# The adaLN gates of a two-layer decoder: broadcast by unit-column matmuls, or written to memory and read back into every partition

## The chip, the cores and the metric

One core of one Trainium2 chip runs the whole program; the other cores idle. The metric is the device time of one execution in microseconds. TensorE (PE in the profile, PEld for its weight loads) multiplies; VectorE (DVE) and ScalarE (ACT) copy, add, scale and split operands; GpSimd (POOL) does gathers and small work; SyncE (SP) issues nearly all loads of weights. A DMA that SP issues stands in one queue of instructions with its waits: while SP waits for one, what stands behind it isn't issued.

## The reference, cut to what matters

There are two layers. In each, a token mixer (layer 0: sparse attention, layer 1: a gated linear recurrence) and then a mixture of 16 experts are added to the residual stream `x` of 512 tokens by 1024 channels. Each of the four sub-layers has its own shift, scale and gate from the conditioning vector `c`:

```
mod = silu(c) @ ada_w[l, s] + ada_b[l, s]      # 3 x 1024 numbers: shift, scale, gate
h   = rms_norm(x, gain) * (1 + scale) + shift
x   = x + gate * mixer(h)                      # gate: one number for each of the 1024 channels
```

The gate has 1024 numbers for the whole sequence, the same for every token. Here a token is a partition, so the gate has to stand in every partition.

## The kernel before

All products are float32 and are made as three products of split operands (`hi`, `lo`): ACT copies the high part (`whi`, `ohi`), DVE subtracts it (`wlo`, `olo`), and PE adds hi·hi, hi·lo and lo·hi.

**Where the gates come from.** `ada_parts(l, s)` (L161) is the matrix product of `c` with `ada_w[l, s]` in six parts of 512 columns, each with a 2 MB load on SP (L88) and 32 matmuls (L181). Parts 4 and 5 are the gate. Their result lies in four partitions (0, 32, 64, 96) of 128 channels each, and DVE adds it to the bias in `gg` (L187). The parts are spread over the mixers as filling work; the next part's weights are loaded when a buffer is free, which a later part's matmuls or a later split decides.

**Where the gates are used.** `mix_out` (L1698) is the output stage of a mixer: `out_proj` (L357) multiplies the mixer's output `ot` by `w_out` (L373 to L375: hi·hi, hi·lo and lo·hi of the splits, for K tiles 0 to 7), four token tiles by two column halves. It begins with K tiles 0 to 6 of token tiles 0 and 1, stops at a `yield`, and gets the gate by `rest.send(...)`. Then comes K tile 7 of tiles 0 and 1, and for each tile of tokens the residual: DVE multiplies the PSUM bank by the gate (`yres`, L406) and adds it to `x` (L407). The splits of token tile 2 (`ohi` on ACT, L367, and `olo` on DVE, L368) reuse the buffers of tile 0, so ACT waits for tile 0's last hi·lo product. Behind the output stage come the norm, the router and the expert lists of the mixture (`route`), and then the experts.

**What makes the broadcast.** `gate_row` (L213) takes one half of a gate: four matmuls, of a unit column of `ident` repeated 128 times by `gg`, put 512 gate values into all 128 partitions of a PSUM tile `gate_ps` (L217; each float32 matmul runs as two, so the trace has 8 for a half). `gate_tokens` (L221) copies the mixer's gate to `gateb`, 128x1024, by two DVE copies (L224). `Moe.gate` (L1425) does it for the gate of the experts and keeps two layouts: `gate64` (DVE, L1435) and `gate32` (ACT, L1437), which the experts' outputs are multiplied by (L1534).

**The order.** `mix_out` first queues the loads of the first expert weights, `m.load(EARLY, m.early)` (L1226 and L1230 on SP), then the first part of `out_proj`, `m.prepare()` (the small matmuls L1194 and L1201), `m.gate()` and `gate_tokens`. A scheduler then orders the instructions of each engine.

Of the kernel before, what the change touches and what calls it, by code (L numbers as in the profile page):

```python
# [9 lines left out]
F32 = mybir.dt.float32  # L10
# [3 lines left out]
AF = mybir.ActivationFunctionType  # L14
# [4 lines left out]
D = 1024  # L19
# [12 lines left out]
EARLY = 3  # L32
# [27 lines left out]
def kernel(ctx: ExitStack, tc: tile.TileContext, I, out, dbg=None, upto="all"):  # L60
    nc = tc.nc
# [5 lines left out]
    dram = ctx.enter_context(tc.tile_pool(name="dram", bufs=1, space=bass.MemoryType.DRAM))  # L67
    psum = ctx.enter_context(tc.tile_pool(name="psum", bufs=1, space=bass.MemoryType.PSUM))

    def sb(name, side="left", bufs=1):  # L70
        return tc.tile_pool(name=name, bufs=bufs, side=side, reuse_waits="tile")

    def mm_ps(name):
        return psum.tile([128, 512], F32, tag="mm", bufs=3, name=name)

    def tp_ps(name):
        return psum.tile([128, 512], F32, tag="tp", bufs=3, name=name)
# [8 lines left out]
    def load_w(src, pool=ring, eng=nc.sync):  # L86
        w = pool.tile([128, 8, 512], F32, tag="w", name="w")
        loads.append(eng.dma_start(out=w, in_=src))  # L88
        return w
# [8 lines left out]
    ident = const.tile([128, 128], F32, name="ident")  # L98
# [45 lines left out]
    def side_by_side(makes):  # L144

        first = last = makes[0]()
        for make in makes[1:]:
            with tc.high_priority(offset=TOGETHER):
                ins = make()
            edge(ins, last)  # L150
            last = ins
        return first
# [3 lines left out]
    gates = {}  # L156
# [4 lines left out]
    def ada_parts(l, s):  # L161

        aw = I["ada_w"][l, s]
        mod = const.tile([128, 16], F32, name=f"mod{l}{s}")
        gg = const.tile([128, 2, 128], F32, name=f"gg{l}{s}")
        mods[l, s] = mod
        gates[l, s] = gg

        def load(t, wpool, eng):
            if t == 4:  # L170
                nc.gpsimd.memset(gg, 0.0)
                nc.scalar.dma_start(out=gg[0:128:32],
                                    in_=bass.AP(tensor=I["ada_b"].tensor,
                                                offset=I["ada_b"].offset + 3 * D * (2 * l + s) + 2 * D,
                                                ap=[[128, 4], [512, 2], [1, 128]]))
            return load_w(aw[:, 512 * t:512 * t + 512].rearrange("(k p) n -> p k n", p=128), wpool, eng)

        def part(t, w):
            ps = mm_ps("ada_ps")
            for q in range(0, NK, 2):  # L180
                side_by_side([lambda k=k, g=g: nc.tensor.matmul(  # L181
                    ps[32 * g:32 * g + 32, 0:128], cond[:, k:k + 1].to_broadcast([128, 32]),
                    w[:, k, 128 * g:128 * g + 128], start=(k == 0), stop=(k == NK - 1))
                    for k in (q, q + 1) for g in range(4)])
                yield
            if t >= 4:
                nc.vector.tensor_add(gg[:, t - 4], gg[:, t - 4], ps[:, 0:128])  # L187
                return
            row = small.tile([128, 128], F32, tag="adarow", bufs=2, name="adarow")
            nc.vector.tensor_copy(row, ps[:, 0:128])  # L190
            tp = tp_ps("ada_tp")
            nc.tensor.transpose(tp[:, 0:128], row, ident)
            b0 = (2 * l + s) * 24 + 4 * t
            m4 = mod[:, 4 * t:4 * t + 4]
            nc.vector.tensor_add(m4, tp[:, 0:128:32], cols[:, b0:b0 + 4])
            if t >= 2:
                g0 = 96 + (2 * l + s) * 8 + 4 * (t - 2)
                nc.vector.scalar_tensor_tensor(m4, m4, 1.0, cols[:, g0:g0 + 4], op0=ALU.add, op1=ALU.mult)

        return [(lambda wpool=ring, eng=nc.sync, t=t: load(t, wpool, eng), lambda w, t=t: part(t, w)) for t in range(6)]  # L200

    def in_turn(parts, ahead, wpool=ring):
# [7 lines left out]
        for part, w in q:  # L210
            yield from part(w)

    def gate_row(gg, t):  # L213

        ps = tp_ps("gate_ps")
        for g in range(4):
            nc.tensor.matmul(ps[:, 128 * g:128 * g + 128], ident[:, 32 * g:32 * g + 1].to_broadcast([128, 128]),  # L217
                             gg[:, t, :], start=True, stop=True)
        return ps

    def gate_tokens(pool, gg):  # L221
        gb = pool.tile([128, D], F32, tag="gateb", bufs=1, name="gateb")
        for t in range(2):
            nc.vector.tensor_copy(gb[:, 512 * t:512 * t + 512], gate_row(gg, t))  # L224
        return gb


# [187 lines left out]
    def nsa(l, load, src, m, ada0, fill):  # L415
        win = I["nsa_w_in"][0]
        with ExitStack() as st:
            with ExitStack() as s2:
                ot, wts = nsa_heads(l, load, win, m, s2, ada0, fill)
            dump("ot", ot)  # L420
            mix_out(l, m, ot, wts, src)
# [472 lines left out]
    def hgrn(l, m0, st0, fill):  # L894
        win = I["hgrn_w_in"][0]
        with ExitStack() as st:
# [31 lines left out]
            def begun(st):  # L928
                st.push(wst)
                return got[0]  # L930

            mix_out(l, m, ot, None, None, begun)
        return m

# [232 lines left out]
    class Moe:  # L1167
# [257 lines left out]
        def gate(self):  # L1425

            self.gate_of = {m: self.pool.tile([128, 8 * m], F32, name=f"gate{m}") for m in (64, 32)}
            for t in range(2):
                ps = gate_row(gates[self.l, 1], t)
                for m, g in self.gate_of.items():  # L1430
                    for j in range(128 // m):
                        if 8 * m * j // 512 == t:
                            r, c = slice(m * j, m * j + m), 8 * m * j % 512
                            if m == 64:
                                nc.vector.tensor_copy(g[r], ps[r, c:c + 8 * m])  # L1435
                            else:
                                nc.scalar.activation(g[r], ps[r, c:c + 8 * m], AF.Copy)  # L1437

        def slot_tokens(self, p):
            if p < PINS:  # L1440
# [260 lines left out]
    def mix_out(l, m, ot, wts, src, front=None):  # L1701

        if src is not None:
            xp = m.under.enter_context(sb("mx"))
            m.x = [xp.tile([128, D], F32, name=f"x{t}") for t in range(NT)]
        m.early = m.left.enter_context(sb("moew0", side="right", bufs=EARLY))
        m.load(EARLY, m.early)
        with ExitStack() as st:
            rest = front(st) if front else out_begin(st, ot, wts)
            wk = st.enter_context(sb("mixo"))  # L1710
            m.work = wk
            m.prepare()
            m.gate()
            rest.send((wk, gate_tokens(wk, gates[l, 0]), src, m.x, m.tokens))
            m.load(2, ring)

    def out_begin(st, ot, wts, scale=None):
        g = out_proj(st.enter_context(sb("mixw")), ot, wts, scale)
        next(g)
        return g  # L1720
# [8 lines left out]
    def moe_out(pool, m, t):  # L1729
# [4 lines left out]
        return m.x[t]  # L1734

    ada = {(l, s): ada_parts(l, s) for l in range(2) for s in range(2)}
    first = ada[0, 0][0:4]
    fill = ada[0, 0][4:6] + ada[0, 1] + ada[1, 0][0:4]
# [90 lines left out]
```

## Time and profile before

| | |
|---|---|
| three runs | 1449.33, 1451.39 and 1454.22 us, median 1451.39 us |
| the profiled execution | 1452.37 us, span 1450.4 us |
| mean granted clock of TensorE | 0.947 of full speed |
| PE busy | 1280.3 us, 88% of the span |
| DVE busy | 714.7 us, 49% |
| ACT busy | 428.9 us, 30% |
| DMA | 346.47 MB, mean 239 GB/s |

Start times are microseconds from the start of the profiled span; the span is 1.97 us shorter than that execution's time. Layer 0's output stage lies at about 419 to 485 us and layer 1's at about 1080 to 1145; the experts of layer 0 run from about 500 us, those of layer 1 from about 1165.

### The profile page before, as it was taken

Reading aid. Unit: us, or ns where it says so; the run is one execution under the profiler, and the core shown is the slowest. Engines: PE = TensorE matmul, PEld = TensorE weight load, DVE = VectorE, ACT = ScalarE, POOL = GpSimd, SP = SyncE. Lnnn points to the kernel's source line nnn. Section 1 sums busy time; section 2 is a strip of 40 time slices with the busy share of each in tenths; the row PEclk is TensorE's granted clock in tenths of the full one; section 3 lists DMA queues with packets and bytes.
Section 4 is the critical chain, followed back from the end, with each engine's and each line's share of the span. In section 5 each row is a group of like instructions: output and inputs, shape, how many; then the busy total and the mean of one; then the engine's idle time right before and its main releaser. Section 6 shows DMA issues by size and latency. Waiting matters only on the chain. (4 is left out here: it accounts for less than half of the span.)

```text
span 1450.4 us, 26217 instructions
## 1 busy us (share of the span) xinstructions
PE 1280.3 (88%) x10634; PEld 773.9 (53%) x10635; DVE 714.7 (49%) x1801; ACT 428.9 (30%) x1007; POOL 154.2 (11%) x174
## 2 busy tenths in 40 slices
PE   5998898988989699999983999999889699999991
PEld 3666655765557443443322867777667533444320
DVE  4435886458846732222217465666555652222213
ACT  3323565336643121111114422233233221111110
POOL 2102212221100100000004100000000110000002
PEclk9999999999999799999995999999889899999996
DMA  9802551734373799999996333353335689999995
GB/s 358 221 1 85 181 187 62 289 123 155 118 315 135 264 339 394 370 374 371 402 364 195 101 105 130 118 175 117 118 117 232 236 312 389 376 378 385 387 387 190
DMA packets 108335, 346.47 MB, mean 239 GB/s; under 512 B 17251, under 2 KB 40635, under 8 KB 87724
## 3 DMA queue, kind: packets, MB, share of 16 engines
q1 hardware_dynamic: 77632, 276.80, 50.9%
q0 software_dynamic: 10048, 38.54, 8.0%
q10 hardware_dynamic: 20524, 29.34, 5.9%
q8 instruction: 87, 1.43, 0.4%
q14 instruction: 44, 0.36, 0.1%
HBM read 320.73 MB, written 23.93 MB: 238 GB/s over the span
## 5 line engine op out<-in xcount | busy, mean ns | idle before, releaser
L1491 PE MATMUL h_ps<-w,hgt 128*32 128x256 f32 (+1 forms) x2240 | 325.5, 492 | 6.5 <-DMA w<-in_moe_w_dram 6.5
L1491 PEld LDWEIGHTS h_ps<-w,hgt 128*32 128x32 f32 (+1 forms) x2240 | 110.8, 124 | 196.8 <-issue 160.5
L1531 PE MATMUL y_ps<-w,gT 128*64 128x512 f32 (+1 forms) x1120 | 158.2, 485 | 1.1 <-ACT gT L1520 1.1
L1509 DVE TENSOR_TENSOR go<-h_ps,g 32x256 f32<-32x256 f32 (+1 forms) x70 | 58.9, 841 | 134.5 <-ACT g L1507 134.2
L313 PE MATMUL pr_ps<-whi,hThi 128*128 128x512 f32 x256 | 107.5, 421 | 2.9 <-DVE qn L518 1.8
L1531 PEld LDWEIGHTS y_ps<-w,gT 128*64 128x64 f32 (+1 forms) x1120 | 55.9, 123 | 89.6 <-issue 75.8
L314 PE MATMUL pr_ps<-wlo,hThi 128*128 128x512 f32 x256 | 102.7, 401 | 0.0
L315 PE MATMUL pr_ps<-whi,hTlo 128*128 128x512 f32 x256 | 102.3, 400 | 0.1
L1534 DVE TENSOR_TENSOR y<-y_ps,gate 128x512 f32<-128x512 f32 (+1 forms) x52 | 31.2, 599 | 136.7 <-PE y_ps L1531 134.1
L1507 ACT ACTIVATE g<-h_ps 64x512 f32<-64x512 f32 (+1 forms) x52 | 26.8, 516 | 229.1 <-PE h_ps L1491 166.6
L303 DVE TENSOR_TENSOR wlo<-w,whi 128x512 fp32r<-128x512 f32 x120 | 80.2, 703 | 23.9 <-ACT whi L302 20.5
L1473 DVE TENSOR_SCALAR hgt<-hg_tp,modp 128x96 f32<-128x96 f32 (+2 forms) x128 | 43.5, 366 | 97.1 <-PE hg_tp L1465 91.6
L302 ACT ACTIVATE whi<-w 128x512 fp32r<-128x512 f32 x120 | 71.9, 631 | 64.6 <-DMA w<-in_nsa_w_in_dram 16.5
L802 ACT ACTIVATE P<-P,nm 128x128 f32<-128x128 f32 (+3 forms) x128 | 71.0, 556 | 38.9 <-DVE nm L800 37.7
L181 PE MATMUL ada_ps<-w,cond 128*32 128x128 f32 x1536 | 64.9, 297 | 15.4 <-DMA w<-in_ada_w_dram 9.6
L796 PE MATMUL s_ps<-kT,qT 128*128 128x256 f32 (+3 forms) x256 | 66.0, 364 | 11.4 <-DVE qn L518 6.9
L800 DVE CUSTOM_DVE_ANT_0 P<-s_ps,tb 128x128 f32<-128x128 f32 (+3 forms) x128 | 59.6, 486 | 22.0 <-PE s_ps L796 18.3
L1520 ACT ACTIVATE gT<-g_tp 128x384 f32<-128x384 f32 (+2 forms) x32 | 14.6, 457 | 165.5 <-PE g_tp L1517 156.8
L1453 POOL DMA_INDIRECT hg<-xnd,gidxp x26 | 23.6, 906 | 363.2 <-PE hg_tp L1465 360.6
L841 PE MATMUL p_tp<-ident,P 128*128 128x128 f32 x320 | 52.7, 282 | 8.1 <-DVE P L816 8.0
L1471 ACT ACTIVATE hgt<-hg_tp,modp 128x96 f32<-128x96 f32 (+2 forms) x128 | 47.9, 420 | 40.6 <-DVE hgt L1473 36.7
L181 PEld LDWEIGHTS ada_ps<-w,cond 128*32 128x32 f32 x1536 | 42.2, 117 | 31.5 <-issue 23.8
(367 smaller groups left out, 2102.9 us busy)
## 6 DMA issues: line engine op xcount, KB each, us to landing
w<-in_moe_w_dram SPq DMA_DIRECT2D x120, 1024.0 KB
w<-in_moe_w_dram SPq DMA_DIRECT2D x32, 2048.0 KB
w<-in_ada_w_dram SPq DMA_DIRECT2D x22, 2048.0 KB
w<-in_hgrn_w_in_dram SPq DMA_DIRECT2D x12, 1024.0 KB
tb<-tabd ACTq DMA_DIRECT2D x16, 456.0 KB
yd<-y ACTq DMA_DIRECT2D x56, 128.0 KB
yd<-zero POOLq DMA_DIRECT2D x12, 512.0 KB, 8.7
w<-in_nsa_w_in_dram SPq DMA_DIRECT2D x8, 512.0 KB
```

The source lines that it names most:

```text
L181: side_by_side([lambda k=k, g=g: nc.tensor.matmul(ps[32 * g:32 * g + 32, 0:128], cond[:, k:k + 1].to_broadcast([128, 32]), w[:, k, 128 * g ...
L302: nc.scalar.activation(a, w[:, k], AF.Copy)
L303: nc.vector.tensor_sub(b, w[:, k], a.bitcast(F32))
L313: nc.tensor.matmul(ps, hi[:, k, c], a, start=(k == 0), stop=False)
L314: nc.tensor.matmul(ps, hi[:, k, c], b, start=False, stop=False)
L315: nc.tensor.matmul(ps, lo[:, k, c], a, start=False, stop=(k == NK - 1))
L796: nc.tensor.matmul(sp[:, :n], qT[:, (hd + j) % 8, 128 * t:128 * t + 128], kT[:, v, br, gl, :n], start=(v == 0), stop=(v == 1))
L800: nc.vector.tensor_tensor_reduce(ps, sp[:, :n], tbs[hd + j][:, 384 - 128 * t:512], scale=-1.0, scalar=3.0e38, op0=ALU.add, op1=ALU.min, ac ...
L802: nc.scalar.activation(ps, ps, AF.Exp, bias=nm[:, i:i + 1], scale=-1.0, accum_out=z[:, i:i + 1])
L1491: self.pe(nc.tensor.matmul(ps[m * j:m * j + m, :w], hgt[:, k, r:r + m], ws[half][:, x + i, c:c + w], start=(k == 0), stop=(k == NK - 1)))
L1509: nc.vector.tensor_mul(go[r:r + m].rearrange("q (f p) -> q p f", f=4)[:, 2 * m * j:2 * m * j + 2 * m], ps[64 + m * j:64 + m * j + m, :w].r ...
L1531: self.pe(nc.tensor.matmul(ps[m * j:m * j + m, :w], gT[:, f, r:r + m], w2v[:, f, w * j:w * j + w], start=(f == 0), stop=(f == 3)))
```

## The change

The result of each gate part is written to a small DRAM tile `gd` by SP right after DVE's add, 4 partitions of 128 values (2 KB). Where a gate is needed in every partition, SP reads it back with a partition step of 0: once for `gateb` (512 KB), six times for the two layouts of the experts' gate (two of 64 partitions by 512 values, four of 32 by 256). `gate_row`, its matmuls and the copies out of PSUM are gone. In `mix_out` both gates now come before the first loads of expert weights in the code.

```diff
@@ ada_parts
         gg = const.tile([128, 2, 128], F32, name=f"gg{l}{s}")
+        gd = dram.tile([2, 4, 128], F32, name=f"gd{l}{s}")
         mods[l, s] = mod
-        gates[l, s] = gg
+        gates[l, s] = gd
...
             if t >= 4:
                 nc.vector.tensor_add(gg[:, t - 4], gg[:, t - 4], ps[:, 0:128])
+                nc.sync.dma_start(out=gd[t - 4], in_=gg[0:128:32, t - 4])
                 return
...
-    def gate_row(gg, t):
-
-        ps = tp_ps("gate_ps")
-        for g in range(4):
-            nc.tensor.matmul(ps[:, 128 * g:128 * g + 128], ident[:, 32 * g:32 * g + 1].to_broadcast([128, 128]),
-                             gg[:, t, :], start=True, stop=True)
-        return ps
-
-    def gate_tokens(pool, gg):
+    def gate_load(dst, gd, c, n):
+
+        nc.sync.dma_start(out=dst, in_=bass.AP(tensor=gd.tensor, offset=gd.offset + c, ap=[[0, dst.shape[0]], [1, n]]))
+
+    def gate_tokens(pool, gd):
         gb = pool.tile([128, D], F32, tag="gateb", bufs=1, name="gateb")
-        for t in range(2):
-            nc.vector.tensor_copy(gb[:, 512 * t:512 * t + 512], gate_row(gg, t))
+        gate_load(gb, gd, 0, D)
         return gb
@@ Moe.gate
             self.gate_of = {m: self.pool.tile([128, 8 * m], F32, name=f"gate{m}") for m in (64, 32)}
-            for t in range(2):
-                ps = gate_row(gates[self.l, 1], t)
-                for m, g in self.gate_of.items():
-                    for j in range(128 // m):
-                        if 8 * m * j // 512 == t:
-                            r, c = slice(m * j, m * j + m), 8 * m * j % 512
-                            if m == 64:
-                                nc.vector.tensor_copy(g[r], ps[r, c:c + 8 * m])
-                            else:
-                                nc.scalar.activation(g[r], ps[r, c:c + 8 * m], AF.Copy)
+            for m, g in self.gate_of.items():
+                for j in range(128 // m):
+                    gate_load(g[m * j:m * j + m], gates[self.l, 1], 8 * m * j, 8 * m)
@@ mix_out
-        m.load(EARLY, m.early)
         with ExitStack() as st:
             rest = front(st) if front else out_begin(st, ot, wts)
             wk = st.enter_context(sb("mixo"))
             m.work = wk
+            gateb = gate_tokens(wk, gates[l, 0])
+            m.gate()
+            m.load(EARLY, m.early)
             m.prepare()
-            m.gate()
-            rest.send((wk, gate_tokens(wk, gates[l, 0]), src, m.x, m.tokens))
+            rest.send((wk, gateb, src, m.x, m.tokens))
             m.load(2, ring)
```

Line numbers of the changed kernel are 3 to 10 lower than those of the kernel before in what follows (L365 is the old L368, L403 the old L406, L1223 the old L1226). Two places show how the engines' order moves. The first is SP late in layer 1's mixer, from the last load of `ada_w` to the loads of expert weights (`moe_w`). Before:

```order
L88 DMA w<-in_ada_w_dram 128x8x512
L88 DMA w<-in_hgrn_w_out_dram 128x8x512 x2
L1226 DMA w<-in_moe_w_dram 128x2048 x6
L1230 DMA w<-in_moe_w_dram 128x4096
L1226 DMA w<-in_moe_w_dram 128x2048 x2
```

After (`gd_117` and `gate_...` belong to the experts' gate of layer 1, `gd_114` and `gateb` to its mixer's gate):

```order
L88 DMA w<-in_ada_w_dram 128x8x512
L189 DMA gd_117<-gg_116 4x128
L88 DMA w<-in_hgrn_w_out_dram 128x8x512
L217 DMA gate_10654<-gd_117 64x512
L217 DMA gate_10655<-gd_117 32x256 x2
L88 DMA w<-in_hgrn_w_out_dram 128x8x512
L189 DMA gd_117<-gg_116 4x128
L217 DMA gate_10654<-gd_117 64x512
L217 DMA gate_10655<-gd_117 32x256 x2
L1223 DMA w<-in_moe_w_dram 128x2048 x2
L217 DMA gateb<-gd_114 128x1024
L1223 DMA w<-in_moe_w_dram 128x2048 x4
```

Two writes and six reads now stand between the last `ada_w` load and the first pair of expert loads, and the read of `gateb` stands behind that pair.

The second is DVE in layer 1's output stage, from the copy of the modulation values to the second half of the weight splits. Before:

```order
L1204 COPY modp<-mp_ps 128x4x4
L368 TENSOR_TENSOR olo<-ot,ohi 128x128 x2
L1435 COPY gate_10698<-gate_ps 64x512 x2
L224 COPY gateb<-gate_ps 128x512 x2
L406 TENSOR_TENSOR yres<-out_ps,gateb 128x512 x2
L407 TENSOR_TENSOR x_4223<-x_4223,yres 128x512
L407 TENSOR_TENSOR x_4224<-x_4224,yres 128x512
L368 TENSOR_TENSOR olo<-ot,ohi 128x1024 x2
```

After:

```order
L1201 COPY modp<-mp_ps 128x4x4
L365 TENSOR_TENSOR olo<-ot,ohi 128x128 x2
L365 TENSOR_TENSOR olo<-ot,ohi 128x1024
L403 TENSOR_TENSOR yres<-out_ps,gateb 128x512 x2
L404 TENSOR_TENSOR x_4231<-x_4231,yres 128x512
L404 TENSOR_TENSOR x_4232<-x_4232,yres 128x512
L365 TENSOR_TENSOR olo<-ot,ohi 128x1024
L403 TENSOR_TENSOR yres<-out_ps,gateb 128x512
L404 TENSOR_TENSOR x_4233<-x_4233,yres 128x512
L303 SCALAR_TENSOR_TENSOR wlo<-w,gain,whi 128x512 x6
```

The four copies are gone, and one of the two splits `olo` of 128x1024 (token tile 2) has moved ahead of the four residual operations. In layer 0 the copies are gone in the same way, but both splits of 128x1024 stay behind the four residual operations.

## Rows read from the trace of the kernel before

**Rows 1.** The groups of instructions of the gates: count, then busy us and mean ns, then idle before.

```profile
L217 PE MATMUL gate_ps<-gg,ident 128*128 128x128 f32 x64 | 7.9, 279 | 0.0
L1437 ACT ACTIVATE gate<-gate_ps 32x256 f32<-32x256 f32 x8 | 3.0, 374 | 15.2 <-DVE gate L1435 15.0
L224 DVE COPY gateb<-gate_ps 128x512 f32<-128x512 f32 x4 | 2.8, 692 | 0.8 <-PE gate_ps L217 0.8
L1435 DVE COPY gate<-gate_ps 64x512 f32<-64x512 f32 x4 | 2.7, 687 | 8.8 <-PE gate_ps L217 8.8
```

**Rows 2.** Timeline of layer 0's output stage: start, duration, engine, instruction, idle before.

```profile
419.20 1.16 PE L217 MATMUL gate_ps<-gg,ident 128*128 128x128 f32 x8
421.94 0.50 PE L373 MATMUL out_ps<-whi,ohi 128*128 128x512 f32 x1 [1.58 <-ACT ohi L367]
...
436.10 2.84 PE L217 MATMUL gate_ps<-gg,ident 128*128 128x128 f32 x24
438.69 0.48 PE L373 MATMUL out_ps<-whi,ohi 128*128 128x512 f32 x1
439.67 1.39 DVE L406 TENSOR_TENSOR yres<-out_ps,gateb 128x512 f32<-128x512 f32 x2
```

**Rows 3.** Timeline of layer 1's output stage.

```profile
1095.95 3.88 PE L217 MATMUL gate_ps<-gg,ident 128*128 128x128 f32 x32
1096.17 0.48 DVE L368 TENSOR_TENSOR olo<-ot,ohi 128x128 fp32r<-128x128 f32 x2
1099.58 0.48 PE L373 MATMUL out_ps<-whi,ohi 128*128 128x512 f32 x1
1100.39 2.01 ACT L367 ACTIVATE ohi<-ot 128x1024 fp32r<-128x1024 f32 x2 [0.86 <-PE out_ps L374]
1100.56 1.39 DVE L406 TENSOR_TENSOR yres<-out_ps,gateb 128x512 f32<-128x512 f32 x2
1103.07 2.35 DVE L368 TENSOR_TENSOR olo<-ot,ohi 128x1024 fp32r<-128x1024 f32 x2
1104.34 0.50 PE L375 MATMUL out_ps<-whi,olo 128*128 128x512 f32 x1 [0.70 <-DVE olo L368]
```

**Rows 4.** Stretches: length, busy time and count per engine, granted clock, DMA share, GB/s.

```profile
142.00:143.00 1.00, 0.00 (x0) 0.00 (x0) 0.00 (x0) 0.00 (x0) 1.00 (x1) 0.96 0.84 241
424.00:428.00 4.00, 3.04 (x7) 2.46 (x8) 3.04 (x7) 1.26 (x4) 0.00 (x0) 0.50 1.10 465
430.00:436.00 6.00, 6.00 (x28) 4.98 (x27) 0.00 (x0) 0.00 (x0) 0.00 (x0) 1.00 1.01 420
440.00:443.40 3.40, 2.25 (x8) 0.97 (x6) 3.39 (x6) 1.50 (x2) 0.00 (x0) 1.00 0.01 2
490.00:510.00 20.00, 10.10 (x88) 5.20 (x89) 18.36 (x105) 3.49 (x10) 6.14 (x7) 0.63 0.79 284
530.00:760.00 230.00, 224.40 (x1640) 86.85 (x1636) 59.13 (x108) 38.56 (x91) 8.94 (x10) 0.99 0.99 381
1082.00:1096.00 14.00, 12.75 (x99) 10.47 (x97) 6.76 (x11) 3.25 (x9) 1.01 (x1) 1.00 0.27 104
```

**Rows 5.** SP's queue in layer 1, and a DMA on ACT's: start, time of the issues.

```profile
1026.25 39.54 SPq L88 DMA_DIRECT2D w<-in_hgrn_w_out_dram  x2
1078.60 17.70 SPq L1226 DMA_DIRECT2D w<-in_moe_w_dram  x6
...
140.36 0.45 ACTq L734 DMA_DIRECT2D tb<-tabd  x1
```

**Rows 6.** SP's waits, 980 to 1100: us in total, times, longest.

```profile
SPq L88 <- PE lvA_ps L1063: 39.0, 2, 35.1
...
SPq L1226 <- DVE wlo L306: 12.7, 1, 12.7
```

**Rows 7.** DMA issues: count, KB each, median us from issue to landing.

```profile
tb<-tabd ACTq DMA_DIRECT2D x16, 456.0 KB
yd<-zero POOLq DMA_DIRECT2D x12, 512.0 KB, 8.7
```

## The prediction

> **What bounds the kernel now.** I read the page's counts first, then the groups of the gates, then the two output stages row by row, since 88% PE busy over the whole span says nothing about one stage. The change touches 64 matmul instances of 7.9 us together, four copies of 692 ns, four of 687 ns and eight of 374 ns [rows 1]. What they cost is decided by where they stand.
>
> In layer 0 the 64 fall into two places [rows 2]. Eight run at 419.20 for 1.16 us, and behind them PE waits until 421.94 for ACT's `ohi`: they stand in a gap and cost nothing. The other 24 run at 436.10, in the middle of the output products, and the next product begins at 438.69. The residual `yres` follows at 439.67, behind the last copy of the gate on DVE.
>
> In layer 1 all 32 run in one block [rows 3], from 1095.95 to the next product at 1099.58. There more follows from it: ACT's `ohi` of token tile 2 starts at 1100.39, when tile 0's last hi·lo product has freed its buffer; DVE does `yres` (1100.56, 1.39 us), two additions to `x`, and only at 1103.07 the `olo` splits; PE gets its first lo·hi product at 1104.34, having waited for `olo`. So the block of gates delays a chain PE, ACT, DVE, PE.
>
> Behind it the chain goes on without slack that I can find: products, residual, norm, router, lists of tokens, first gather. In 490 to 510 the DMA engines are at 0.79 and DVE is busy for 18.36 of 20 us; the stream of expert weights is full only later, 0.99 in 530 to 760, with PE busy for 224.40 of 230 us [rows 4]. The stream starts with the end of the route, so an earlier route should start it earlier.
>
> **What is removed.** Layer 0: 438.69 − 436.10 = 2.6 us of PE ahead of K tile 7. DVE's copies hang on the same matmuls: `yres` starts 0.98 us behind the product of 438.69, and of that lag the three products of K tile 7 need most, so I take 2.6 us and nothing more. The eight matmuls at 419.20 give 0: with them gone PE waits for `ohi` from 419.2 instead of 420.4.
>
> Layer 1: the gates alone give 1099.58 − 1095.95 = 3.6 us. The order adds to it, since DVE now splits tile 2 ahead of the residual. K tile 7 starts at about 1095.95; its first hi·lo product is done some 0.8 us later (as 1100.39 stands to 1099.58), so `ohi` of tile 2 is ready at 1096.75 + 2.01/2 = 1097.8, `olo` at 1097.8 + 2.35/2 = 1099.0, and PE's first lo·hi product starts there instead of at 1104.34: 5.3 us earlier. Of PE's work on tile 2, six products ran ahead of 1104.34 and only two will run ahead of 1099.0; four products at full clock take 4 × 6.00/28 = 0.9 us [rows 4]. That leaves 4.4 us. DVE then has `yres`, `x` and the second `olo` to do while PE runs the other 22 products of tile 2, 22 × 0.214 = 4.7 us, against 1.39 + 1.3 + 1.2 = 3.9 us: it keeps up. Bounds: 3.5 us (the order gives nothing, and `olo` of K tile 7, done at 1096.65, holds PE for a moment) and 4.6 us.
>
> **What is added on SP.** 22 DMAs, each about 0.4 us of issue (0.45 in the row of `tb`) [rows 5], some 10 us spread over the program, on an engine that mostly waits. Each write waits for DVE's add, which comes right behind the part's matmuls; the weight load queued behind it waits for a later part's matmuls or for a split in any case. In layer 1, ahead of the second half of `w_out`, SP waits 35.1 us for PE, and ahead of the first pair of expert loads 12.7 us for DVE's `wlo` [rows 6].
>
> What a read must wait for its write is in no row: nothing here is written to memory by SP and read back at once. Bounds: 0, and the 8.7 us of a 512 KB write on GpSimd's queue [rows 7], 256 times as large; a 2 KB write is nearer to the lower end, and I take 2 to 3 us as an estimate between the two. Twice in each layer a set of three reads waits so. In layer 1 the first set lies in the wait of 35.1 us; the second write is issued at about 1065.8 (the two loads of `w_out` end their issue at 1026.25 + 39.54) and even with 8.7 us its reads go at 1074.5, ahead of 1078.60 when the expert loads may start [rows 5]. In layer 0 the sets stand between loads of `ada_w` that wait far longer. So the price is 0; without cover it would be 2 to 3 us four times.
>
> [...]
>
> **What the read of `gateb` costs.** Nearest row: a `tb` read of 456 KB, also many partitions over the same small table; two were issued by 140.36, the engines moved 241 GB/s at 0.84 share in 142 to 143 [rows 4, 5, 7]. At that rate 512 KB take 2.2 us. In layer 0 it is issued at about 402 and needed at 437. In layer 1 it stands behind the pair of expert loads of 1078.60: 2 MB at 381 GB/s are 5.5 us, plus its own 2.2 and some latency: landed by about 1088, needed at 1097. The engines are at 0.27 between 1082 and 1096 [rows 4]. Price 0, with 9 us of cover. All the reads move 0.9 MB a layer, 2.4 us at 381 GB/s, none of it in the full stream of the experts.
>
> **The clock.** TensorE ran at half clock in 424 to 428, where seven products took 3.04 us, against 28 in 6.00 us at full clock: 0.43 − 0.21 = 0.22 us for each product. In the thin stretch behind the gates of layer 0 (2.25 busy of 3.40 us) the clock stayed at 1.00 [rows 4]. The removal doesn't thin that stretch, it moves it forward; layer 1's becomes shorter. I take 0. The wait before 421.94 grows by 1.2 us, and the half clock that follows it may begin or end elsewhere: 15 products ran through it, so at most ±3.3 us.
>
> **Sum.** 1452.37 − 2.6 − 4.4 = 1445.4 us for the profiled execution. That one is 1.0 us above the median, so beside the median of 1451.39 it is 1444.4. I forecast 1445.
>
> **Rivals.** What can be told from no change here is about 0.3%, 4.4 us.
>
> *The gain is used up on the way.* The route starts earlier, but the experts end with their stream of weights, and this depends on when buffers come free; or the phase of the clock in 490 to 510 (0.63 granted) shifts and takes a part. For it: 0.99 of DMA share in 530 to 760. Against: 0.79 in 490 to 510. If half is lost: 1452.4 − 3.5 = 1448.9, or about 1448 on the median's scale. Chance 0.27.
>
> *Slower: the clock falls in the thin stretches.* Without the gates' dense matmuls ahead of them, both stretches of waiting (440 to 443.4, and the one that will stand at 1097 to 1099) would be followed by products at half clock. To turn a gain of 7.0 into a loss of over 4.4 it must cost 11.4 us, 52 products at half clock, 26 in each layer; the fall at 422 lasted 15. With 15 in each it would cost 6.6 us and end level with before, 1452. It decides from 52 on, 1456 or more. Chance 0.08 for that. [...]
>
> *`gateb` is late in layer 1.* It would have to land after 1097. If the read waited like the next expert loads and landed 3 us late, the gain would be 4 us: 1448. This, too, ends within 0.3%; I count it in the 0.27 above.
>
> *More than 9 us.* A half clock stretch vanishes with the shift, in 422 to 429 or at the experts' start: 1452.4 − 7.0 − 3.3 = 1442. Chance 0.08.
>
> **Numbers.** My forecast (4.4 to 9 us faster) has 0.57, more than 9 us 0.08: faster by over 0.3% 0.65, within 0.3% 0.27, slower 0.08. The range goes from 1441 (the full 7.0, and 3.3 of clock) to 1451 (nearly all used up); the forecast's own range is 1443 to 1447.
>
> **What the profile after would show.** Right: no `gate_ps`; in layer 0 K tile 7 follows K tile 6 without a gap and `yres` stands 2.6 us nearer to the products' start; in layer 1 the first lo·hi product of tile 2 comes some 3 us behind K tile 7's start instead of 4.8 behind it plus the gates' 3.6; both routes and the first expert products come 2.6 and then 7 us earlier; SP's loads of `w_out` and of the first experts stand where they stood. Wrong: DVE waits for a DMA at `yres`; PE waits for a load of `ada_w` or `w_out`; the granted clock is under 1.00 in either thin stretch; or the first expert product is earlier and the last isn't.

## The result and the profile after

| | before | after |
|---|---|---|
| median of 8 runs | 1449.92 us (1446.14 to 1455.36) | 1437.74 us (1436.55 to 1442.73) |
| ratio | | 0.9916, 95% interval 0.9899 to 0.9933 |
| profiled execution, span | 1450.4 us | 1434.9 us |

The change takes 12.2 us off, 0.84%, where 6 to 7 were forecast; 1437.7 lies below the range of 1441 to 1451. Of that, 1.5 us are the starting point: the prediction had the median of three runs of the kernel before, 1451.39, and over eight runs it is 1449.92. The two profiles differ by 15.5 us, since the one of before was slower than its median and the other a little faster.

The page of the changed kernel, busy times by engine:

```profile
PE 1267.9 (88%) x10570; PEld 766.7 (53%) x10571; DVE 708.5 (49%) x1793; ACT 425.8 (30%) x999; POOL 154.8 (11%) x174
```

That is 64 matmuls, 64 weight loads and 8 DVE and 8 ACT copies fewer. To see where the time went I took the same VectorE instruction in both profiles and subtracted its start times. The difference grows in four places; the other stretches move by up to 1.7 us either way (868 to 900 gains that much) and nearly cancel:

| stretch (times of before) | what runs there | gained |
|---|---|---|
| 419 to 486 | layer 0's output stage and route | 2.7 us |
| 842 to 868 | layer 1's mixer | 3.6 us |
| 1024 to 1056 | layer 1's mixer | 4.5 us |
| 1094 to 1150 | layer 1's output stage | 4.4 us |

The first and the last are the two terms of the forecast. Layer 0's output stage after the change, as a timeline, beside [rows 2] (L370 to L372 are the old L373 to L375; in the rows further down L182 is the old L181):

```profile
435.97 0.39 PE L370 MATMUL out_ps<-whi,ohi 128*128 128x512 f32 x1
436.85 1.37 DVE L403 TENSOR_TENSOR yres<-out_ps,gateb 128x512 f32<-128x512 f32 x2 [9.97 <-PE out_ps L372]
440.61 0.50 PE L372 MATMUL out_ps<-whi,olo 128*128 128x512 f32 x1 [0.73 <-DVE olo L365]
```

`yres` now waits for the product and for nothing else; it starts 2.8 us earlier (436.85 for 439.67). Layer 1's, beside [rows 3]:

```profile
1084.35 0.50 PE L370 MATMUL out_ps<-whi,ohi 128*128 128x512 f32 x1
1084.44 0.48 DVE L365 TENSOR_TENSOR olo<-ot,ohi 128x128 fp32r<-128x128 f32 x2
1085.15 1.06 ACT L364 ACTIVATE ohi<-ot 128x1024 fp32r<-128x1024 f32 x1 [0.65 <-PE out_ps L371]
1086.24 1.22 DVE L365 TENSOR_TENSOR olo<-ot,ohi 128x1024 fp32r<-128x1024 f32 x1 [1.32 <-ACT ohi L364]
1087.38 1.28 DVE L403 TENSOR_TENSOR yres<-out_ps,gateb 128x512 f32<-128x512 f32 x2
1087.52 0.80 PE L372 MATMUL out_ps<-whi,olo 128*128 128x512 f32 x1
```

K tile 7 starts at 1084.35 and tile 2's first lo·hi product 3.2 us later; before it was 8.4 us from the gates' start to that product.

The other two gains, 8.1 us, lie in the mixer of layer 1, where the change touches no computation. There the timeline of PE's weight loads (PEld) shows this in the kernel before:

```profile
848.54 0.36 PEld L181 LDWEIGHTS ada_ps<-w,cond 128*32 128x32 f32 x13 [1.79 <-issue]
...
1029.55 0.32 PEld L1063 LDWEIGHTS lvA_ps<-Q,K 128*32 128x32 f32 x22
1030.60 0.19 PEld L181 LDWEIGHTS ada_ps<-w,cond 128*32 128x32 f32 x5 [0.73 <-DMA w<-in_ada_w_dram]
1034.72 0.61 PEld L181 LDWEIGHTS ada_ps<-w,cond 128*32 128x32 f32 x11 [3.94 <-issue]
```

and this in the changed one:

```profile
1023.62 0.63 PEld L182 LDWEIGHTS ada_ps<-w,cond 128*32 128x32 f32 x16 [1.55 <-DMA w<-in_ada_w_dram]
```

A run of 16 weight loads, which all need the same tile of `ada_w`, is cut into 5 and 11. Between them no weight load starts for 3.9 us, and PE waits for no semaphore ("issue"); its matmuls stand for 3.5 us. The stretches of the kernel before around it (length, busy time of PE, PEld, DVE, ACT, POOL, granted clock, DMA share, GB/s):

```profile
1026.00:1030.00 4.00, 2.19 (x168) 1.81 (x160) 3.74 (x10) 0.25 (x1) 1.01 (x1) 1.00 1.01 374
1030.00:1032.00 2.00, 0.64 (x5) 0.19 (x5) 1.87 (x5) 0.00 (x0) 0.00 (x0) 0.59 0.99 358
1032.00:1034.00 2.00, 0.00 (x0) 0.00 (x0) 0.00 (x0) 0.00 (x0) 0.00 (x0) 0.50 1.05 388
1034.00:1036.00 2.00, 1.27 (x12) 0.83 (x13) 0.00 (x0) 0.00 (x0) 0.00 (x0) 0.50 0.60 223
1036.00:1040.00 4.00, 4.00 (x10) 3.14 (x11) 0.00 (x0) 0.00 (x0) 0.00 (x0) 0.50 0.01 5
```

No engine does anything in 1032 to 1034; the DMA engines are full, and the clock that was 1.00 to 1030 falls to 0.50 and stays there to 1040. The changed kernel in the same piece of program:

```profile
1022.00:1026.00 4.00, 2.56 (x39) 1.83 (x26) 2.07 (x6) 0.00 (x0) 0.00 (x0) 0.68 1.03 372
1026.00:1032.00 6.00, 6.00 (x56) 4.21 (x55) 2.81 (x5) 0.60 (x1) 0.00 (x0) 0.93 0.37 117
```

Among the DMA queues of the page of before (packets, MB, share of the engines) is one of the kind "instruction", whose packets move while the kernel runs:

```profile
q8 instruction: 87, 1.43, 0.4%
```

That is 16.4 KB a packet. I take them for PE's program. The experiments below give 256 instructions for one, so 64 bytes for an instruction, and 1.43 MB are then 22,300 of them (an estimate from these numbers): PE's 10,634 matmuls and 10,635 weight loads, and 1,000 more that the page doesn't count. (The count doesn't follow the number of instructions alone: the changed kernel, with 128 fewer, has 88 packets. Why is not shown.) In the trace of before one of these packets moves from 1032.24 to 1033.34, inside the wait, and PE goes on 1.4 us later, at 1034.72. At the other wait one moves from 846.00 to 847.11, and PE goes on at 848.54. Theory D: the 64 PE instructions that are gone from layer 0 have moved the later ones against the blocks in which the program is fetched, and so removed these waits and the half clock behind them. Rivals: theory A, the earlier start alone changes where the clock falls; theory B, accidents of one execution; theory C, the new writes on SP push a load back that delays `ada_w`.

### The profile page after: what moved, and what is told of

It is laid out like the page before. It is cut to its first block, busy times and chain, and to the rows that moved or that the text cites. A ratio compares the mean times of both kernels' runs of the same rounds, so it can differ in the third digit from the quotient of the medians.

```text
span 1434.9 us, 26103 instructions
## 1 busy us (share of the span) xinstructions
PE 1267.9 (88%) x10570; PEld 766.7 (53%) x10571; DVE 708.5 (49%) x1793; ACT 425.8 (30%) x999; POOL 154.8 (11%) x174
## 5 line engine op out<-in xcount | busy, mean ns | idle before, releaser
L182 PE MATMUL ada_ps<-w,cond 128*32 128x128 f32 x1536 | 63.4, 295 | 10.7 <-DMA w<-in_ada_w_dram 10.3
L793 PEld LDWEIGHTS s_ps<-kT,qT 128*128 128x128 f32 x256 | 41.1, 197 | 32.8 <-issue 16.4
```

The lines of the kernel that those rows point to most:

```text
L182: side_by_side([lambda k=k, g=g: nc.tensor.matmul(ps[32 * g:32 * g + 32, 0:128], cond[:, k:k + 1].to_broadcast([128, 32]), w[:, k, 128 * g ...
L793: nc.tensor.matmul(sp[:, :n], qT[:, (hd + j) % 8, 128 * t:128 * t + 128], kT[:, v, br, gl, :n], start=(v == 0), stop=(v == 1))
```

## The experiments

Each was compared with the kernel before on the same chip. Its median there was 1450.2 to 1451.7 us, from 11 to 23 runs. Medians below are of 4 to 12 runs unless said otherwise; a second figure is the ratio to the kernel before with its 95% interval. Runs on other chips than the change's are set beside its 1437.7 as they are; the table further down takes the same chip's kernel before off each.

**Second profiles of both kernels.**

> The kernel before, unchanged, for a second profile. Theory A (the two mixers' parts of the gain, 3.5 us at 857 to 866 and 4.5 us at 1041 to 1052 of the first profile, follow from where the work falls and come every time): the same half-clock stretches at the same places as in the first profile, span within 1 us of 1450.4. Theory B (they are accidents of one execution): at least one of the two stretches is missing, and the span is 3 to 5 us shorter.

> The changed kernel, unchanged, for a second profile. Theory A: both stretches of the mixer in layer 1 run as in its first profile, span within 1 us of 1434.9. Theory B: one of them has lost 3 to 5 us.

Measured, one execution each: 1443.44 us (span 1441.5) and 1439.15 us (span 1437.3). The wait at 1031 was there in the second profile of before (5 and 11, 3.82 us) and not in that of the change, but in before the clock was back at full earlier: 1024 to 1056 took 1.7 us less, 842 to 868 1.8 us less. So theory B holds for the clock's part, which comes and goes, not for the wait. Another 3.8 of the 8.9 us by which this profile is shorter come ahead of 400 us, so the whole time of one profile says little.

**One layer alone.** The gates of a layer go by memory only where the pair stands in a set.

```diff
+BY_DMA = {(0, 0), (0, 1)}          # or {(1, 0), (1, 1)}
...
+        if (l, s) in BY_DMA:
+            gd = dram.tile([2, 4, 128], F32, name=f"gd{l}{s}")
+        gates[l, s] = gd if (l, s) in BY_DMA else gg
```

> Gates of layer 0 by memory, those of layer 1 by matmuls as before. Theory A (time is taken from the two output stages, and the shift of 3 us alone changes where the mixer of layer 1 meets the slow clock): 2.9 us in layer 0's output stage, none in layer 1's, and the 4 to 8 us of the mixer as in the whole change: 7 to 11 us in all. Theory C (the 4.5 us of the mixer come from the writes and reads of layer 1's gates, which stand between SP's loads there): 3 to 4 us for the experts' and mixer's shift alone, about 3 us in all.

> Gates of layer 1 by memory, those of layer 0 by matmuls as before. Theory A: 4 us from layer 1's output stage and nothing elsewhere, 4 us in all. Theory C: these 4 us and the 4.5 us at 1028 to 1052, with the load of the output weights 1 us later behind SP's write: 8 to 9 us in all.

Measured: layer 0 alone 1439.89 us, 0.9929 (0.9913 to 0.9945), 11 us faster; layer 1 alone 1445.03 us, 0.9963 (0.9949 to 0.9977), 6 us faster. With layer 0 alone the 5 and 11 is gone, though SP's queue in layer 1 is as before; with layer 1 alone, writes and all, it is there (3.00 us). Theory C falls. Theory A had layer 0's 7 to 11 us in advance, and D, which was not on record yet, fits them too; layer 1's 6 us lie between A's 4 and C's 8 to 9.

**PE instructions added.** The 16 small matmuls L1201 of one layer are done again into the same place, with the same values: 64 PE instructions a time, 0.67 us, in layer 0 in the gap at 419 to 422.

```diff
-            for i in range(4):
+            for i in [i for _ in range(2 if self.l == 0 else 1) for i in range(4)]:
                 for g in range(4):
                     nc.tensor.matmul(pp[32 * g:32 * g + 32, 4 * i:4 * i + 4], ident[:, i::4], self.mod[:, g::4],
```

> The whole change, and in layer 0 the 16 small matmuls of the modulation (L1198) are done twice, with the same result: 64 more PE instructions (32 weight loads, 32 matmuls, 0.67 us), in a gap where PE waits 2.7 us for ScalarE, so that every later PE instruction has the place in PE's program that it had before the change, up to layer 1's gates. Theory D (removing layer 0's 64 gate instructions moved the places at which PE's program is fetched, and so removed two waits of PE without a releaser in the mixer of layer 1, at 1031 and 847, with the half clock behind them): the two waits are back, PE's ada_ps matmuls split as 5 and 11, and the time is 5 to 8 us longer than the change's, 1443 to 1446. Theory A (the gain in the mixer follows from the shift in time alone): within 1 us of the change, 1437 to 1439.

Measured: 1442.90 us, 0.9940 (0.9925 to 0.9956): 5.2 us above the change (3.4 us by the two differences to the kernel before on the same chip), and the cut run of weight loads is back:

```profile
1025.27 0.15 PEld L182 LDWEIGHTS ada_ps<-w,cond 128*32 128x32 f32 x6 [0.52 <-DMA w<-in_ada_w_dram]
1029.57 0.57 PEld L182 LDWEIGHTS ada_ps<-w,cond 128*32 128x32 f32 x10 [4.15 <-issue]
```

The output stages kept their gains (2.8 and 4.4 us).

> The kernel before, with all its gate matmuls, and in layer 0 the 16 small matmuls of the modulation done four times: 192 more PE instructions, 2 us of PE work. If PE's program is fetched in blocks of 256 instructions (16 KB a fetch in the trace's instruction queue, 64 bytes each), later instructions then lie against the blocks as in the changed kernel. Theory D: the waits at 847 and 1031 are gone; in spite of more work the kernel is 4 to 8 us faster than before, 1443 to 1447. Theory A: 0 to 1 us slower than before.

> The kernel before with the small matmuls of layer 0's modulation done five times: 256 more PE instructions, 64 more (0.67 us) than with 192, and otherwise the same order. Theory D: 256 is a whole block, so later instructions lie against the blocks as in the kernel before: the split 5 and 11 and the wait at 1031 are back, and the time is 1450 to 1453, 8 to 10 us above that with 192 more. Theory A: 0.7 us above it, 1442 to 1443.

Measured: with 192 more 1441.99 us, 0.9937 (0.9922 to 0.9953); with 256 more 1452.42 us, 1.0016 (1.0004 to 1.0028). On every engine the two programs differ by these 64 instructions alone. First 192, then 256:

```profile
1025.25 0.57 PEld L181 LDWEIGHTS ada_ps<-w,cond 128*32 128x32 f32 x16 [1.47 <-DMA w<-in_ada_w_dram]
```

```profile
1027.92 0.14 PEld L181 LDWEIGHTS ada_ps<-w,cond 128*32 128x32 f32 x5 [0.45 <-DMA w<-in_ada_w_dram]
1032.89 0.61 PEld L181 LDWEIGHTS ada_ps<-w,cond 128*32 128x32 f32 x11 [4.82 <-issue]
```

A kernel that does more work is 9 us faster, and with 64 instructions more on top it is no faster at all. Some of the 10 us between the two lie elsewhere: with 256 more a second wait of the same kind, 3.1 us, stands in layer 0 at 419 to 422, between two gate matmuls, and layer 0's output stage takes 1.4 us longer than with 192. In the two stretches of the mixer of layer 1 they differ by 5.8 us.

The wait follows the place in every profile. PE's idle time put down to "issue" at `ada_ps` is 3.9 to 5.0 us in the six profiles of programs in which the mixer of layer 1 lies against the blocks as before, the new writes included (`gd_writes_alone` below), and 0 in the seven in which it lies as in the changed kernel. In each of the six a packet of the program lands inside the wait (1027 to 1033), and PE goes on 1.36 to 1.41 us behind it. This decides for theory D. The place of 192 more is that of 64 fewer and the place of 256 more is that of before, while the places of 64 and 128 more (the changed kernel with 128 and 192 more, below) are like neither: that gives the block, 256 instructions.

> Layer 1's gates by memory and layer 0's by matmuls, with 192 more PE instructions in layer 0, so that the mixer of layer 1 lies against the blocks as in the changed kernel. Theory D: no wait at 847 and 1031, 6 us less than the same kernel without the 192 (1445.0), that is 1438 to 1440; against the kernel before with 192 more (1442.0) it shows layer 1's own part, 2 to 5 us. Theory A: 1445 to 1446.

Measured: 1438.98 us, 0.9924 (0.9906 to 0.9943), 6.0 us less than without the 192. Theory D, without a wait at 847 or 1031.

> The whole change, with the small matmuls of layer 0 done three times: 128 more PE instructions, 1.3 us in the gap of 2.7 us. Theory D: the waits without a releaser stand at other places than in either kernel; no sign can be told ahead, the time lies between 1436 and 1446. Theory A: within 1 us of the change.

> The whole change with 192 more PE instructions in layer 0: the fourth place against the blocks. Theory D: between 1435 and 1446, and under 1437 if this place meets no wait at all, which would be a version faster than both kernels. Theory A: within 1 us of the change's 1437.7.

Measured: 1437.49 us, 0.9912 (0.9896 to 0.9928), and 1441.26 us, 0.9937 (0.9919 to 0.9956). Both have a shorter wait of the same kind, 1.5 and 1.6 us at 1024, and in both PE goes on 1.3 to 1.4 us after a packet has landed. None of the four places against the blocks beats the change clearly.

> The whole change, and the small matmuls of the modulation done twice in layer 1 instead: 64 more PE instructions in its output stage, 0.67 us of PE at about 1082, which puts layer 1's experts against the fetched blocks as with layer 0's gates alone removed. Theory D has nothing to lose in the mixer, which lies ahead: 0.3 to 0.7 us slower than the change for the PE work, 1438 to 1439, and up to 2 us either way if the experts of layer 1 meet such waits. Theory A: the same 0.3 to 0.7 us.

> The whole change with 128 more PE instructions in layer 1's output stage (1.3 us of PE), behind the mixer. With 64 more there the median was 1436.4. Theory D: the mixer as in the change; the experts of layer 1 lie against the blocks as in the kernel before; 1437 to 1439, by 0.7 us of PE work above that with 64. Theory A: the same.

Measured: 1436.38 us, 0.9900 (0.9884 to 0.9917), and 1437.33 us, 0.9907 (0.9891 to 0.9924). Behind the mixer the place matters little; the first is the lowest median of all and 1.6 us under what was expected, but not told apart from the change.

**What holds the fetch up.** The first 2 MB of the output weights are loaded later:

```diff
+        with tc.issue_after(behind.ins):      # ScalarE's copy at 1042
+            w0 = load(0, nc.scalar)
```

> The kernel before, with the first 2 MB of layer 1's output weights loaded some 16 us later, from ScalarE's queue behind the copy at 1042, so that in 1026 to 1034 only the load of ada_w is under way. PE's instructions up to there are the same and lie against the blocks as before. Theory E (PE's next block of program waits among the 4 MB of weights that are under way): the wait without a releaser at 1031, 3.5 us, is gone or under 1.5 us, and PE's own wait for ada_w too. Theory F (the block is asked for too late and takes that long with idle DMA engines too): the wait stays at 3 to 4 us. The scheduler moves the split of those weights behind, so the whole time says little: 1444 to 1456.

Measured: 1452.12 us, 1.0013 (0.9993 to 1.0032). The wait is shorter, not gone; its row and the stretch in which it ends:

```profile
1030.96 0.61 PEld L181 LDWEIGHTS ada_ps<-w,cond 128*32 128x32 f32 x11 [1.61 <-issue]
```

```profile
1030.00:1032.00 2.00, 1.03 (x12) 0.60 (x12) 0.57 (x2) 0.00 (x0) 0.00 (x0) 0.50 0.00 0
```

So 2.3 of the 3.9 us hang on the second load, and 1.6 us are left with the DMA engines idle at the end (PE's wait for `ada_w` is left too, 0.6 us). The packet shows both parts. In before it starts to move 1.45 us after the fifth weight load has ended, here 0.83 us ahead of that (1028.52, for a load that ends at 1029.35): that is the 2.3 us. And from its landing at 1029.61 PE takes 1.35 us to go on, as in the profiles with both loads under way. Theory E holds for the larger part, F for the rest. The 2.3 us are of one pair of profiles; the full wait was 3.0 to 4.8 us in six. The stretch to 1056 gained 3 us by it; the split of those weights then came late, and between 1056 and 1094 it lost 4.8.

> The changed kernel with the same later load. It has no wait without a releaser there to lose, only PE's 1.4 us for ada_w and the half clock behind it. Theory E and F alike: these are gone; 1 to 3 us faster than the change if the later split costs nothing (1435 to 1437), else up to 5 us slower.

Measured: 1441.59 us, 0.9943 (0.9924 to 0.9962), 3.9 us above the change: 0.4 us gained at 1024 to 1056, where PE still waits 1.1 us for `ada_w` and not 0 as both theories had it, and 5.4 us lost by the late split.

> The kernel before with all its gate matmuls, and the eight writes of the gates to memory added on SP, with nothing reading them. My prediction's price for them is 0: within 1.5 us of the kernel before. Theory C (the writes hold back the output weights' load by 0.9 us and so let ada_w land earlier): 3 to 5 us faster, with the wait at 1031 shortened.

Measured: 1449.26 us, 0.9994 (0.9982 to 1.0006), with the wait at 4.12 us. The writes cost nothing and give nothing.

## Why the prediction was wrong

In short: the two terms of the sum measured what was forecast, and the sum left out a third, the place of PE's later program.

**Direction and the named steps were right.** Layer 0's 24 instances: 2.6 us forecast, 2.7 measured. Layer 1's block with the moved split: 4.4 forecast, 4.4 measured, 4.8 in the change's second profile. The eight matmuls at 419 gave nothing, as said: `ohi` is waited for 2.67 us instead of 1.58. One reading is off without effect: layer 0 has 32 of the 64 matmul instances, the eight and the 24, and layer 1 the other 32.

**The added DMAs were free**, as said, but one price was mis-sized. SP's waits in the changed kernel in 300 to 480, and in 1050 to 1085 (time, count, longest):

```profile
SPq L217 <- DMA gd<-gg: 14.2, 2, 7.1
...
SPq L217 <- DMA gd<-gg: 6.9, 1, 6.9
```

A read waits 7 us for its write of 2 KB, not 2 to 3; the four sets held SP for 23.5 us together. What the estimate lacked is the load just ahead in SP's queue:

```profile
1053.13 0.39 SPq L88 DMA_DIRECT2D w<-in_hgrn_w_out_dram  x1
1053.56 0.50 SPq L189 DMA_DIRECT2D gd<-gg  x1
1060.98 1.58 SPq L217 DMA_DIRECT2D gate<-gd  x3
```

By the trace's records of packets, 1019 of the 1024 packets of that 2 MB load moved first, the write's four packets at 1060.23 to 1060.33, and the read went 0.65 us later. The 7 us lay near the upper bound, the 8.7 us of [rows 7]; by that bound the cover was enough, and it was: the expert loads' pair went at 1066.30, 12.3 us earlier like all around it, and `gateb` behind it at 1067.25, with `yres` never waiting for a DMA.

**The clock** fell where I put no fall: in layer 1's thin stretch it was 0.72 in 1084 to 1090 (1.00 in its second profile). It cost little: the stage gained 4.4 us with it and 4.8 without.

**The step that failed is the sum.** "1452.37 − 2.6 − 4.4" counts what the gate instructions cost where they stand. It holds nothing for their being part of PE's program: every PE instruction behind layer 0's gates moved by 64 against the blocks of 256, and with that two waits and some of the half clock behind them went, 8.0 us in the first pair of profiles and 4.3 in the second. My fourth rival let half clock vanish "with the shift", for 3.3 us; a wait that goes away in a stage that the diff doesn't touch was never priced. That the gain came out over 9 us, as in this rival, is luck: its mechanism isn't what happened. The experiments give both parts as a table, each median less that of the kernel before on the same chip, in us:

| | place in layer 1's mixer as before | as after |
|---|---|---|
| gates by matmuls | 0 (with 256 more: +2.2) | −9.7 (192 more) |
| layer 1's by memory | −6.1 | −11.3 (192 more) |
| all by memory | −8.8 (64 more) | −12.2 |

Down a column the gates give 8.8 and 2.5 us, 5.6 in the mean, beside the 7.0 forecast; across a row the place gives 9.7, 5.2 and 3.4, 6.1 in the mean. From corner to corner either way adds up to the 12.2 by the table's build, so the medians show that both parts are there and not how large each is; the difference of the two columns stays unexplained.

The profiles divide it better. Layer 0's output stage gained 2.7 to 3.4 us in all nine profiles with its gates by memory, layer 1's 3.5 to 4.9 us in all ten with its own by memory; elsewhere both lie between −1.2 and 0.8. The two stretches of the mixer together are 7.8 to 9.5 us shorter than in the first profile of before in the seven profiles with the place as after, and 0.4 to 3.5 us shorter in the other five with the place as before. In the means the place is worth 6 to 7 us in these two stretches, and the two output stages fit the 7.0 forecast for the gates alone.

**The trace of before had the rows.** I read the waits of the stages that the change touches and the totals of the rest. PE's waits over the whole span have just two put down to "issue", 1.5 and 3.5 us (1.79 and 3.94 us for PEld), both inside a run of equal instructions that all use one tile already loaded, so that no later wait should cut it. They couldn't tell whether the change would remove them: that takes the count of PE instructions ahead of them. But they made a rival of 4 to 9 us of either sign.

**Still open:** what fills the 1.35 to 1.41 us between the landing of a packet and PE's next instruction, and why the packet moves so late. At 847 PE goes on 1.2 to 1.4 us behind a packet as well; whether a load holds that packet up was not tried.

## What to carry to other kernels

When an edit adds or removes tens of instructions on an engine, look in the whole trace for idle time that nothing releases, above all inside a run of equal instructions while the DMA engines are full; price it as a rival of either sign. To tell such a gain from the edit's own, put as many harmless instructions back (or fill up to 256, the block of these runs) and time that too: here 192 more instructions "improved" the kernel by 9 us, and an edit that happened to shift PE's program by as much would have been credited with it. Read a gain stage by stage, from the same instruction in both traces, before believing its sum.

## What the hardware showed that was not expected

- PE's program, as I read the instruction queue of the page of before (87 packets, 1.43 MB), came in packets of 16.4 KB, and the place of the code against blocks of 256 instructions moved 3 to 10 us of 1450 by the medians: 1441.99 us with 192 PE instructions more than before, 1452.42 with 256 more. In the mixer of layer 1 it was a wait of 3 to 4.8 us of PE's weight loads in the six profiles with the place as before and both loads of weights under way, and 1.6 us with one load less beside it. In all seven PE went on 1.35 to 1.41 us after the packet had landed.
- That wait is followed by matmuls at half clock (0.50 granted in 1032 to 1040), so that 3.9 us of waiting cost 4.5 us in the first pair of profiles. In the second, where the clock was back at 1.00 from 1033 (weight loads of the products 0.23 us apart instead of 0.43), the stretch differed by 2.7 us.
- A 2 KB write to memory held the read behind it on SP for 7 us three times and 2.4 us once. It was not the write's own cost: each stood behind a 2 MB load on SP's queue, 0.4 to 1.2 us behind it in the three and 4.4 us in the fourth, and its four packets began to move only when 962 to 1019 of the load's 1024 had, 6.8 to 8.1 us after the load was issued. The read then went 0.65 to 0.71 us behind the last of the four. A write with no load just ahead of it, issued at 857.06 in the changed kernel, had its four packets moved by 858.37, 1.3 us later.
